# Gated delta rule on Trainium2: the old sample states of two head pairs meet their keys and queries in one visit to the tensor engine

## The chip, the cores and the metric

The kernel runs on one core of one Trainium2 chip. The metric is device time in microseconds (us) of one execution; the time before is the median of three runs, 2125.45 us (2124.71 to 2126.7). A profiled execution, from which every duration below is taken, is a run of its own.

## The reference, cut to what matters

One inference step of a one-layer hybrid decoder: 256 prompt tokens of one sequence, and 8 sample sequences of 8 tokens each. Both go through one large input projection (2048 to more than 23,000 columns), then through a gated delta rule (16 key heads, 32 value heads, state 128 x 128 for each value head) and, beside it, a sparse attention; the two are merged, projected and added to the input. The change lies in the delta rule, in the part for the sample sequences. Each of the 8 sequences brings a state S for each of 32 value heads (`state_gdn`, 8 x 32 x 128 x 128 numbers), and per chunk of tokens

```python
u = u_c - einsum('bhck,bhkv->bhcv', w_c, s)          # old state times (weighted) keys
o = einsum('bhck,bhkv->bhcv', qd_c, s) + einsum('bhij,bhjv->bhiv', qk_c, u)   # old state times queries
s = s * gt_c[..., None, None] + einsum('bhck,bhcv->bhkv', kt_c, u)
```

The products of the old state `s` with keys and with queries are what the change moves.

## The kernel before, in words

**The stream.** Nearly all the work is the multiplication of the weights of the big projections with the 320 tokens. A unit is half of the contraction (1024 of 2048) for 128 output columns. Its weights are loaded into `raw`, split by ScalarE into a rounded high part `whi` and by VectorE into the rest `wlo` (`split_ahead`, two units ahead), and multiplied by TensorE in `stream`: 16 products with `whi` (with the high and low part of the tokens in turn), then 8 with `wlo`, each 128 x 128 weights against 320 tokens. The stream's sums lie in two banks of PSUM called `pm`.

**The side work.** All else is written as Python generators. `stream` calls `side_round` twice per unit: after 12 of its 24 products, and at its end. A round steps through the list of generators once, in the order in which they were spawned; each step issues some instructions and yields. The program is thus one fixed order of instructions for each engine, settled when it is built. What decides whether a generator is stepped is a planner's clock: `Clock.cost` gives each instruction a duration, and each engine has a time.

```python
for side in list(self.sides):
    if self.pe_ns - start > limit:
        break
    if side[1] <= clock.t["tensor"]:
        self.step(side)
```

A generator that yields nothing is stepped again when the planner's tensor clock has passed the end of what it issued last, one that yields a time when that is passed. A round ends when its steps have put more than 1800 ns of products on TensorE (`pe_ns`: in `mm`, the columns of the right side divided by 2.4, times 4 for F32). A generator that takes a bank for side work (`ps`, six of them, one of which is lent to the convolution throughout this stage) goes through `need`, which also waits until a bank is idle by the planner's clock. Where a unit needs a buffer that a generator still holds, `force` runs rounds without the stream, and in these rounds banks aren't waited for.

**The recurrent stage.** The heads go by in 8 groups. A group has two head pairs; a head pair `h` is one key head with the value heads 2h and 2h+1. For each group the stream computes keys, queries, gates and values; `kq_gen` and `inverse` build the triangular inverses `XT` of the group (GpSimd works on the inverse while the stream has gone on to the next group). Then, for each head pair, four generators are in the list in this order: `v_gen` (values turned to token-major `vt`), `prompt_chain` (five steps on 256 prompt tokens), `sample_chain` and `norm_gen` (the norm over both chains' outputs `ot`, then the output gate). `G` is what the group's generators share, `K` that of a head pair. `G["T"]` appears when the group's inverse is there, and until then all chains wait.

**`sample_chain` before** (line 2144), once `G["T"]` and `vt` are there: it waits for the state tile `S` (8 sequences x 2 value heads, one DMA per value head; two such tiles in all), `vt` and `XT`; takes a bank and a tile `wt`; step 1 issues eight products, for the sequence pairs j = 0 to 3 and the parity pp of the sequence, of `R` (128 x 32: keys and queries of one sequence, the places of the other parity zero) with the state (128 x 256, both value heads). They fill partitions 32j to 32j+31 of the bank, columns 0 to 255. Two VectorE operations then form `xr` in place (`vt[:, 2]`) out of the bank, the decay `neG` and the values. Step 2 multiplies `xr` by the inverse, into the sample's part of `ot` and into `wt`. Step 3 needs four banks: products of keys with `wt`, and 16 VectorE operations that renew the state. Step 4 stores the state and gives back the tiles; when both chains of a pair have ended, `vt` is free for `v_gen` of the next group.

Below, P0 and S0 are the prompt and sample chain of a group's first head pair, P1 and S1 those of the second, and a figure behind the dot is the step: S1.3 is the state's renewal for the second pair.

In the profile each operation has the line of the common wrapper (L64), so tiles tell groups apart: `ps<-S,R` are the products that the change moves, `ps<-vt,XT` those with the inverse, `ps<-w,kq` the prompt chain's third step, `ps<-w,ktok 32*128` the renewal's products, `S<-S,gtr,ps` the renewal on VectorE. An F32 product stands as two records.

Of the kernel before, what the change touches and what calls it, by code (L numbers as in the profile page):

```python
# [12 lines left out]
OP = mybir.AluOpType  # L13
# [192 lines left out]
class Kernel:  # L206
# [1937 lines left out]
    def sample_chain(self, h, G):  # L2144
        nc, i, o = self.nc, self.i, self.o
        e, hv, K = h % 2, 2 * h, self.K[h]
        R = K["R"]
        yield from self.need(self.S)
        S = self.S.get()
        yield self.idle(S)  # L2150
        for v in range(2):
            nc.sync.dma_start(S[:, :, v, :], i["state_gdn"][0, :, hv + v].rearrange("b k v -> k b v"))
        while "T" not in G or "vt" not in K:
            yield
        vt, kt, XT = K["vt"], K["ktok"], G["XT"]
        s, stl = self.scal(G, e)
        yield self.ready(S, vt, XT)
        yield from self.need(self.ps_side)
        yield from self.need(self.w)
        xr, wt = vt[:, 2], self.w.get()  # L2160
        p = self.psum()
        for pp in range(2):
            for j in range(4):
                self.mm(p[32 * j:32 * j + 32, 0:256], R[:, 1 + pp, 32 * j:32 * j + 32], S[:, 2 * j + pp],
                        start=(pp == 0), stop=(pp == 1), skip=True)
        self.R.put(R)
        for v in range(2):
            self.stt(xr[:, v, :], p[:, 128 * v:128 * v + 128], self.neG[:, 2, hv + v:hv + v + 1], vt[:, 2, v, :],
                     OP.mult, OP.add)
        self.ps_side.put(p)  # L2170
        yield
        yield from self.need(self.ps_side)
        if "ot" not in K:
            yield from self.need(self.ot)
            K["ot"] = self.ot.get()
        ot = K["ot"]
        p = self.psum()
        for v in range(2):
            self.mm(p[:, 128 * v:128 * v + 128], XT[:, 8 + 2 * e + v, :], xr[:, v, :])
        self.act(ot[:, 2], p[:, 0:256].rearrange("p (v d) -> p v d", v=2))  # L2180
        for v in range(2):
            self.ts(wt[:, v, :], p[:, 128 * v:128 * v + 128], stl(v, 2), None, OP.mult)
        self.ps_side.put(p)
        self.drop_T(G)
        yield
        yield from self.need(self.ps_side, 4)
        ps = [self.psum() for _ in range(4)]
        for pp in range(2):
            for j in range(4):
                self.mm(ps[j][:, 256 * pp:256 * pp + 256], kt[32 * j:32 * j + 32, 2 + pp, :], wt[32 * j:32 * j + 32])  # L2190
        for j in range(4):
            for pp in range(2):
                for v in range(2):
                    bb = 2 * j + pp
                    self.stt(S[:, bb, v, :], S[:, bb, v, :], self.gtr[:, bb, hv + v:hv + v + 1],
                             ps[j][:, 256 * pp + 128 * v:256 * pp + 128 * v + 128], OP.mult, OP.add)
            self.ps_side.put(ps[j])
        yield
        for v in range(2):
            nc.sync.dma_start(o[10][0, :, hv + v].rearrange("b k v -> k b v"), S[:, :, v, :])  # L2200
        self.S.put(S)
        self.w.put(wt)
        self.drop_vt(K)
        K["S"] = True
# [296 lines left out]
```

## Time and profile before

| | before |
|---|---|
| median of 3 runs | 2125.45 us (2124.71 to 2126.7) |
| the profiled execution's own time | 2124.4 us |
| its span (first to last instruction) | 2122.7 us, mean granted TensorE clock 0.997 |
| VectorE, ScalarE, GpSimd busy | 67%, 47%, 22% of the span |
| recurrent chains, first to last state product | 878.3 to 1621.8 us |

The span is 1.7 us less than that execution's own time. In a row of the chip's profile "busy" is the time in which an engine has an instruction under way, "idle before" the idle time of the engine just ahead of the instructions of that row, with what ended it. Records of TensorE overlap, since products are pipelined; how fast they follow each other is read from their starts in the timeline.

### The profile page before, as it was taken

What the parts mean: (1) busy time and instruction counts of PE and PEld (TensorE: products, weight loads), DVE (VectorE), ACT (ScalarE), POOL (GpSimd) and SP (SyncE); (2) the same over time, 40 slices, a digit from 0 to 9 for tenths busy, and PEclk for the clock granted to TensorE, in tenths of its full rate; (3) what the DMA queues carried; (4) which work ended last, traced back from release to release, by engine and by line L of the source; (5) the groups of instructions that cost most, each with busy time, mean ns of one, the idle gap of its engine ahead of it and who ended that gap; (6) DMA issues with size and microseconds to landing.
All of it is one profiled execution on the core that took longest, in us unless ns stands there. A gap on an engine that the chain in (4) does not pass through costs nothing.

```text
span 2122.7 us, 44819 instructions
## 1 busy us (share of the span) xinstructions
PE 2093.0 (99%) x17513; PEld 2013.7 (95%) x17513; DVE 1421.5 (67%) x2900; ACT 987.5 (47%) x2253; POOL 464.3 (22%) x653
## 2 busy tenths in 40 slices
PE   7999999999999999999999999999999999999997
PEld 7999999999999999899999999999999999999997
DVE  4776655889855577777878787878666545455443
ACT  3225465333343455474747464646445534333343
POOL 2001000000001108361818181818080000000000
PEclk9999999999999999999999999999999999999998
DMA  9996663996688677686878686868687867555562
GB/s 347 333 335 179 190 177 99 289 282 183 164 240 249 197 191 202 160 235 182 226 181 228 176 232 172 232 171 228 170 246 215 246 203 210 172 152 152 161 182 81
DMA packets 713987, 438.96 MB, mean 207 GB/s; under 512 B 73936, under 2 KB 697136, under 8 KB 711472
## 3 DMA queue, kind: packets, MB, share of 16 engines
q1 hardware_dynamic: 709696, 413.45, 69.0%
q0 software_dynamic: 3616, 21.02, 2.9%
q8 instruction: 137, 2.24, 0.5%
q10 hardware_dynamic: 464, 1.65, 0.2%
q14 instruction: 74, 0.61, 0.1%
HBM read 386.81 MB, written 48.94 MB: 205 GB/s over the span
## 4 chain that ended last, share of the span: by engine, by line
PE 73%; issue 22%; DVE 2%; DMA 1%; ACT 1%; SPq 1%; DVEq 0%; POOL 0%; POOLq 0%; ACTq 0%
PE pm L64 57%; PE ps L64 16%; DMA raw<-in_w_in_dram 1%; SPq L64 1%; DVE S L64 1%; DMA rawx<-in_w_ada_dram 1%; DVE wlo L64 1%; ACT ot L64 0%; ACT whi L64 0%; DVE sga L64 0%; DVE y1l L64 0%; DVEq L2497 0%; DVE w L64 0%; DVE awl L64 0%; ACT ps L64 0%
## 5 line engine op out<-in xcount | busy, mean ns | idle before, releaser
L64 PE MATMUL pm<-xh,whi 128*128 128x320 f32 (+1 forms) x3108 | 943.5, 318 | 2.3 <-DVE qiS L64 1.3
L64 PE MATMUL pm<-xl,whi 128*128 128x320 f32 (+1 forms) x3108 | 910.4, 307 | 0.1
L64 DVE TENSOR_TENSOR wlo<-raw,whi 128x1024 fp32r<-128x1024 f32 x466 | 579.1, 1252 | 274.5 <-ACT whi L64 261.9
L64 PEld LDWEIGHTS pm<-xh,whi 128*128 128x128 f32 x3108 | 584.5, 188 | 29.8 <-issue 22.4
L64 PEld LDWEIGHTS pm<-xl,whi 128*128 128x128 f32 x3108 | 585.1, 188 | 1.3 <-DVE xl L64 0.3
L64 ACT ACTIVATE whi<-raw 128x1024 fp32r<-128x1024 f32 x466 | 489.4, 1058 | 170.6 <-PE pm L64 105.1
L64 PE MATMUL pm<-xh,wlo 128*128 128x320 f32 (+1 forms) x3108 | 521.2, 307 | 0.5 <-DVE wlo L64 0.5
L64 PEld LDWEIGHTS pm<-xh,wlo 128*128 128x128 f32 x3108 | 469.4, 188 | 1.0 <-DVE wlo L64 1.0
L64 POOL TENSOR_TENSOR X<-X,tmpx 48x31 f32<-48x31 f32 (+15 forms) x248 | 175.3, 707 | 19.4
L64 POOL TENSOR_TENSOR tmpx<-blk,X 48x31 f32<-48x31 f32 (+15 forms) x248 | 161.0, 649 | 52.3 <-DMA blk<-d_b 34.1
L64 DVE SCALAR_TENSOR_TENSOR ps<-xp,cs,ps 128x344 f32<-128x344 f32 x192 | 111.5, 581 | 6.8
L64 POOL TENSOR_TENSOR sc<-sc,mh 128x6 f32<-128x6 f32 (+1 forms) x24 | 44.4, 1848 | 276.8 <-DVE sc L64 193.7
L64 PE MATMUL pm<-y1h,whi 128*128 128x320 f32 x336 | 99.5, 309 | 1.4 <-ACT whi L64 0.9
L64 POOL TENSOR_TENSOR rfin<-rfin,mh 128x3 f32<-128x3 f32 x1 | 0.8, 849 | 455.1 <-DVE rfin L64 455.1
L64 PE MATMUL pm<-y1l,whi 128*128 128x320 f32 x336 | 99.2, 307 | 0.0
L64 DVE SCALAR_TENSOR_TENSOR S<-S,gtr,ps 128x128 f32<-128x128 f32 x256 | 67.4, 341 | 0.1
L64 PEld LDWEIGHTS pm<-y1h,whi 128*128 128x128 f32 x336 | 63.0, 187 | 1.9 <-ACT whi L64 1.9
L64 PE MATMUL ps<-xh,whi 128*128 128x320 f32 (+1 forms) x220 | 64.7, 309 | 0.0
L64 ACT ACTIVATE xp<-pm 128x256 f32<-128x256 f32 (+1 forms) x128 | 32.1, 304 | 70.1 <-PE pm L64 69.9
L64 ACT ACTIVATE ot<-ot,sc 128x128 f32<-128x128 f32 x96 | 29.9, 390 | 73.5 <-DVE sc L64 73.5
L64 PE MATMUL ps<-xl,whi 128*128 128x320 f32 (+1 forms) x220 | 63.7, 304 | 0.0
L64 PEld LDWEIGHTS pm<-y1l,whi 128*128 128x128 f32 x336 | 63.0, 187 | 0.0
(405 smaller groups left out, 2791.2 us busy)
## 6 DMA issues: line engine op xcount, KB each, us to landing
raw<-in_w_in_dram SPq DMA_DIRECT2D x328, 512.0 KB
raw<-in_w_pa_dram SPq DMA_DIRECT2D x64, 512.0 KB
rawx<-in_w_ada_dram SPq DMA_DIRECT2D x18, 1024.0 KB
a<-in_w_ada_dram SPq DMA_DIRECT2D x16, 1024.0 KB
S<-in_state_gdn_dram SPq DMA_DIRECT2D x32, 512.0 KB
out_dram<-S SPq DMA_DIRECT2D x32, 512.0 KB
raw<-in_w_pb_dram SPq DMA_DIRECT2D x32, 512.0 KB
raw<-in_w_out_dram SPq DMA_DIRECT2D x32, 512.0 KB
```

The source lines that it names most:

```text
L64: made = fn(*args, **kw)
```

## The change

Both sample chains of a group enter themselves in a list, `G["SR"]`. The first then waits for a flag, `G["xr"]`. The second waits for both state tiles and a bank, issues the eight products of the first pair into columns 0 to 255 of the bank and those of the second into columns 256 to 511, then the four VectorE operations that form both `xr`, and sets the flag. After it each chain yields until its `xr` is ready (one yield more than before), and only then takes `wt` and goes on to step 2. The number of products, of VectorE operations and of DMAs is what it was; a bank is taken once per group for them and no longer twice.

```diff
-        yield self.ready(S, vt, XT)
-        yield from self.need(self.ps_side)
+        xr = vt[:, 2]
+        G.setdefault("SR", []).append((hv, R, S, vt))
+        if len(G["SR"]) == 2:
+            yield self.ready(vt, XT, *(x[2] for x in G["SR"]))
+            yield from self.need(self.ps_side)
+            p = self.psum()
+            for c, (_, r, sv, _) in zip((0, 256), G["SR"]):
+                for pp in range(2):
+                    for j in range(4):
+                        self.mm(p[32 * j:32 * j + 32, c:c + 256], r[:, 1 + pp, 32 * j:32 * j + 32], sv[:, 2 * j + pp],
+                                start=(pp == 0), stop=(pp == 1), skip=True)
+                self.R.put(r)
+            for c, (h0, _, _, vv) in zip((0, 256), G["SR"]):
+                for v in range(2):
+                    self.stt(vv[:, 2, v, :], p[:, c + 128 * v:c + 128 * v + 128], self.neG[:, 2, h0 + v:h0 + v + 1],
+                             vv[:, 2, v, :], OP.mult, OP.add)
+            self.ps_side.put(p)
+            G["xr"] = True
+            yield
+        while "xr" not in G:
+            yield
+        yield self.ready(xr)
         yield from self.need(self.w)
-        xr, wt = vt[:, 2], self.w.get()
-        p = self.psum()
-        for pp in range(2):
-            for j in range(4):
-                self.mm(p[32 * j:32 * j + 32, 0:256], R[:, 1 + pp, 32 * j:32 * j + 32], S[:, 2 * j + pp],
-                        start=(pp == 0), stop=(pp == 1), skip=True)
-        self.R.put(R)
-        for v in range(2):
-            self.stt(xr[:, v, :], p[:, 128 * v:128 * v + 128], self.neG[:, 2, hv + v:hv + v + 1], vt[:, 2, v, :],
-                     OP.mult, OP.add)
-        self.ps_side.put(p)
-        yield
+        wt = self.w.get()
         yield from self.need(self.ps_side)
```

## The prediction

> **What bounds the kernel now.** I read the page first: busy shares, then the chain of work that ended last.
>
> ```profile
> span 2122.7 us, 44819 instructions
> PE 2093.0 (99%) x17513; PEld 2013.7 (95%) x17513; DVE 1421.5 (67%) x2900; ACT 987.5 (47%) x2253; POOL 464.3 (22%) x653
> PE 73%; issue 22%; DVE 2%; DMA 1%; ACT 1%; SPq 1%; DVEq 0%; POOL 0%; POOLq 0%; ACTq 0%
> ```
>
> TensorE is the bound: 99% busy, and other engines hold 2% of the chain or less each ("issue" is TensorE taking up its next instruction). A change is worth what it takes off TensorE's queue, plus the moments in which TensorE waits. Next, the table by stretches: the first 30 us of the chains of the second and of the last group.
>
> ```profile
> core 0: us, PE busy (x) PEld busy (x) DVE busy (x) ACT busy (x) POOL busy (x), PEclk, DMA share, GB/s
> 977.00:1007.00 30.00, 30.00 (x240) 26.98 (x239) 25.58 (x75) 14.46 (x44) 5.41 (x14) 1.00 0.64 171
> 1615.00:1645.00 30.00, 30.00 (x239) 27.06 (x238) 23.50 (x71) 17.08 (x43) 1.74 (x1) 1.00 0.77 235
> ```
>
> TensorE has no free moment there, and VectorE with 25.6 of 30 us is second, close enough to be watched. The third view is the groups of instructions:
>
> ```profile
> L64 PE MATMUL ps<-S,R 128*32 128x256 f32 x256 | 17.1, 385 | 0.0
> ```
>
> 256 records are 128 products, 16 visits of eight. 17.1 us is all that they are busy, so even their removal would be 0.8% of the run; they are only regrouped. "Busy" doesn't show what a visit costs, though: for that I take TensorE's timeline, the first group's two visits.
>
> ```profile
> 877.78 0.60 PE L64 MATMUL ps<-vt,XT 128*128 128x128 f32 x4
> 878.32 1.07 PE L64 MATMUL ps<-S,R 128*32 128x256 f32 x16
> 879.32 0.42 PE L64 MATMUL pm<-xh,whi 128*128 128x320 f32 x1
> 879.57 0.31 PE L64 MATMUL pm<-xl,whi 128*128 128x320 f32 x1
> ...
> 881.04 0.31 PE L64 MATMUL pm<-xl,whi 128*128 128x320 f32 x1
> 881.18 0.59 PE L64 MATMUL ps<-w,ktok 128*128 128x256 f32 x2
> 881.61 0.61 PE L64 MATMUL ps<-vt,PT 128*128 128x128 f32 x4
> 882.06 1.06 PE L64 MATMUL ps<-vt,XT 128*128 128x128 f32 x8
> 883.04 1.07 PE L64 MATMUL ps<-S,R 128*32 128x256 f32 x16
> 884.04 0.41 PE L64 MATMUL pm<-xh,whi 128*128 128x320 f32 x1
> 884.30 0.31 PE L64 MATMUL pm<-xl,whi 128*128 128x320 f32 x1
> ```
>
> Prices from starts: the stream makes ten products from 879.57 to 881.04, 0.147 us each. Two records of 256 columns take 881.18 to 881.61, 0.216 each; four of 128 columns 881.61 to 882.06, 0.11 each.
>
> **What a visit of the state products costs.** From the first `vt,XT` (877.78) to the second product of the resumed stream (879.57) are 1.79 us. Four records of 128 columns (0.44) and one of the stream (0.147) leave 1.20 for the state products. In the second visit: 884.30 less 882.06 is 2.24, less eight records (0.88), less 0.147, leaves 1.21. What should they take? Their products use 32 columns of the array, so four run side by side, and narrow windows of the timeline show that they start in fours:
>
> ```profile
> 878.32 0.42 PE L64 MATMUL ps<-S,R 128*32 128x256 f32 x4
> 878.56 0.61 PE L64 MATMUL ps<-S,R 128*32 128x256 f32 x8
> 878.77 0.61 PE L64 MATMUL ps<-S,R 128*32 128x256 f32 x8
> ```
>
> The fours start at 878.32, 878.56 and 878.77, some 0.22 apart, the pace of one 256-column record, and that with other weights each time. Four fours at 0.216 are 0.86. So 0.34 us of each visit is a surcharge for going into the 32-column form and out of it: a late start (878.32, where the fourth `vt,XT` record would end at 878.22), a late return, and 0.25 instead of 0.147 to the stream's second product. Is it paid by any interruption of the stream? No:
>
> ```profile
> 895.04 0.31 PE L64 MATMUL pm<-xl,whi 128*128 128x320 f32 x1
> 895.18 1.02 PE L64 MATMUL ps<-w,kq 128*128 128x256 f32 x4
> 895.86 0.50 PE L64 MATMUL pm<-xh,whi 128*128 128x320 f32 x1
> 896.19 0.30 PE L64 MATMUL pm<-xl,whi 128*128 128x320 f32 x1
> ```
>
> From 895.18 to 896.19 are 1.01; less 0.147 that is 0.86, four records at 0.216 and nothing over. Full-width side work interrupts the stream for free; the narrow form is what costs.
>
> **The change part by part.** *Merged visit.* All 16 products now follow each other: eight fours at 0.216 (1.73) and one surcharge (0.34), 2.07 in place of 2.41. Saved: 0.34 a group, 2.7 us over 8 groups. Bounds: nothing, if going from the first pair's half to the second's costs a surcharge too; 2.5 if the fours' own pace of 0.22 is taken. I take 2.7, since fours already follow each other at that pace from one sequence to the next.
>
> [...]
>
> *When it is issued.* In the first round (877.78) the old order was P0.1, S0.1, and then the round's 1800 ns were used up (eight products count 3413), so P1.1 and S1.1 came a round later (882.06, 883.04). Now S0 issues nothing, so P1.1 (427) follows P0.1 (427), and S1 issues the merged visit, all in the first round. Its conditions hold there: inverse and values are the same for both pairs, and the states were loaded long before. The first pair's VectorE operations wait for the whole visit, 0.86 later; nothing of that pair is due before the next round anyway.
>
> *What follows.* The added yield puts S0.2 one round later, into the third with P0.3 and P1.3. Then: fourth round P0.4, S0.3; fifth P0.5, P1.4, S1.2; sixth P1.5 and, if four banks are free, S1.3. Before, it took nine rounds. Fewer rounds save nothing by themselves (above), but the chains end some 5 to 8 us sooner: a round is 12 products (1.76) and the side work. VectorE's and ScalarE's operations are as many as before, the DMAs too; SyncE's state loads and stores only move with the chains. The later `wt` and the two `R` tiles given back together hold nobody up.
>
> *The stall in the first group.* Here something late today may come early enough:
>
> ```profile
> 898.77 1.15 PE L64 MATMUL ps<-w,ktok 32*128 32x256 f32 x16
> 901.11 0.44 PE L64 MATMUL ps<-ident,vf 128*128 128x128 f32 x2 [0.53 <-DVE S L64]
> 902.14 0.66 PE L64 MATMUL ps<-ident,vf 128*128 128x128 f32 x4 [0.60 <-DVE S L64]
> ```
>
> The stream needs a value buffer, `force` runs the side work alone, S1.3 goes out (898.77), and `v_gen` of the next group waits twice for VectorE to empty S1.3's banks: 1.13 us. `v_gen` needed `vt` of the first pair, free only after P0.5 in this same round. With P0.5 two rounds sooner nothing need be forced. I take the 1.13; bounds are 0 and the same again, if the early order only moves the forced rounds elsewhere.
>
> *The sum.* 2.7 and 1.1 are 3.8 us off the profiled execution's own 2124.4: 2120.6. The median of the runs shown is 1.05 above that execution, so in the median's terms 2125.45 - 3.8 = 2121.6, or 0.18% less. A measurement of this kernel tells about 0.2% (4.25 us) from no change.
>
> **Rivals.** *More stalls go (faster by over 0.2%).* Two later waits of TensorE have ScalarE late with `whi`, behind a norm's operations:
>
> ```profile
> 1550.57 0.41 PE L64 MATMUL pm<-xh,whi 128*128 128x320 f32 x1 [0.30 <-ACT whi L64]
> 1654.33 0.41 PE L64 MATMUL pm<-y1h,whi 128*128 128x320 f32 x1 [0.87 <-ACT whi L64]
> ```
>
> Norms follow chains, so chains that end sooner may take both away: 3.8 + 1.2 = 5.0, 2120.4. For it: both rows name a `whi` that stands behind a norm on ScalarE, and the norm would go earlier. Against: an order that is new everywhere may put its own waits there.
>
> *VectorE is overrun (slower).* Before, the renewals S0.3 and S1.3 were 14.5 us apart, now about 7:
>
> ```profile
> 986.87 1.15 PE L64 MATMUL ps<-w,ktok 32*128 32x256 f32 x16
> 1001.33 1.15 PE L64 MATMUL ps<-w,ktok 32*128 32x256 f32 x16
> 983.24 1.20 DVE L64 TENSOR_SCALAR w<-ps,sc 128x128 f32<-128x128 f32 x4 [2.58 <-ACT ot L64]
> 988.16 4.21 DVE L64 SCALAR_TENSOR_TENSOR S<-S,gtr,ps 128x128 f32<-128x128 f32 x16
> 1004.42 4.22 DVE L64 SCALAR_TENSOR_TENSOR S<-S,gtr,ps 128x128 f32<-128x128 f32 x16
> 1010.37 1.87 ACT L64 ACTIVATE ot<-ot,sc 128x128 f32<-128x128 f32 x6 [5.36 <-DVE sc L64]
> 1013.21 1.05 ACT L64 ACTIVATE whi<-raw 128x1024 fp32r<-128x1024 f32 x1
> 1014.60 0.31 PE L64 MATMUL pm<-xh,whi 128*128 128x320 f32 x1
> ```
>
> The place is the norm after S1.3: ScalarE waits 5.36 us for VectorE's small operation, which stands behind the renewal, and `whi` behind that ends (1014.26) only 0.34 before TensorE needs it (1014.60). VectorE, busy 25.6 of 30, has some 1.0 us free in 7; 4.2 of renewal is then 3.2 us late. If half of that reaches `whi`, 1.6 less 0.34 is 1.3 us of stall in each of 8 groups: 10 - 2.7, 2132.8. It begins to cost from 0.34 us of delay on, and shows as slower from (4.25 + 2.7) / 8 = 0.87 of stall a group. Against it: the work moves forward, into VectorE's idle time (2.58 at 983.24), and at that time ScalarE waits for VectorE, so an earlier renewal also lets the norm go earlier. [...] In the visit itself the rows speak against it: four operations after 2.07 us of products, at the renewal's pace (4.21 for 16) 1.1 us.
>
> *Only the surcharge goes:* 2.7, 2122.75. *It doesn't do what it says:* the halves pay a surcharge each, or S1 isn't ready in the first round and nothing else shifts: 2125.45 at worst.
>
> **How the numbers follow.** Forecast case 0.40; only the surcharge 0.16; more stalls gone 0.30; nothing saved 0.06; VectorE overrun 0.08. The forecast lies 0.45 us short of the bound, and the runs shown spread over 2 us, so I count 0.06 of its 0.40 as faster by over 0.2%: faster 0.36, same 0.56, slower 0.08. The range reaches on the one side to the case of more stalls, with the second bound of the forced rounds (2120.4 - 1.1, so 2119.3), on the other to nothing saved and one us of spread, 2126.5.
>
> **What would show it right or wrong.** In the profile after, `ps<-S,R` must stand in the timeline as x32, eight times, with 2.07 us between the end of full-width work and the resumed pace; 2.4 would show a surcharge between the halves. Ahead of it should stand eight `vt,XT` records, of P0.1 and P1.1. `ident,vf` should have no idle time before it. VectorE overrun would show as idle time of `pm<-xh,whi` or `pm<-xh,wlo` after `whi` or `wlo`, group after group some 35 us after the visit. I am wrong in the step of the rounds if chains end no sooner, and in the main term if the span changes by less than 2 us with every wait as it was.

## The result, and the profile after

| | before | after |
|---|---|---|
| median | 2126.15 us (2124.71 to 2127.02, 6 runs) | 2140.11 us (2139.16 to 2140.67, 6 runs) |
| span of the profiled execution | 2122.7 us | 2137.5 us |
| granted clock, mean | 0.997 | 0.995 |

The change makes the kernel slower by 14.0 us: ratio 1.0066, 95% interval 1.0057 to 1.0076. The forecast was 2121.6 us, the range 2119.3 to 2126.5; the result lies outside it, on the other side.

The page of the kernel after, its head and the shares of the chain of work that ended last:

```profile
span 2137.5 us, 44793 instructions
PE 2099.1 (98%) x17513; PEld 2021.3 (95%) x17513; DVE 1421.6 (67%) x2900; ACT 987.5 (46%) x2253; POOL 463.6 (22%) x653
PE 66%; issue 22%; DVE 6%; DMA 3%; ACT 2%; SPq 1%; DVEq 0%; POOL 0%; POOLq 0%; ACTq 0%
```

The counts of TensorE's, VectorE's, ScalarE's and GpSimd's instructions are those of before to the last one, and VectorE is busy as long. No work was added. What changed is the chain: VectorE holds 6% of it in place of 2%, DMA 3% in place of 1%. TensorE now waits for others.

**The merged visit** is there, eight times. The first group's, in TensorE's timeline of the kernel after (start, duration, engine, line, operation, records):

```profile
878.15 1.05 PE L64 MATMUL ps<-vt,XT 128*128 128x128 f32 x8
879.13 1.93 PE L64 MATMUL ps<-S,R 128*32 128x256 f32 x32
880.99 0.41 PE L64 MATMUL pm<-xh,whi 128*128 128x320 f32 x1
881.24 0.31 PE L64 MATMUL pm<-xl,whi 128*128 128x320 f32 x1
```

From 878.15 to 881.24 are 3.09 us; eight records at 0.11 and one of the stream (0.147) taken off leave 2.06. The price was 2.07, and the other seven visits come to the same.

**The waits of TensorE** in the stage (from 740 us to its end), of the kernel after: who waits, for whom, us in all, how often, the longest.

```profile
PE pm L64 <- ACT whi L64: 7.6, 6, 2.6
PE ps L64 <- DMA cst<-in_conv_w_dram: 2.5, 2, 2.3
PE ps L64 <- DVE S L64: 1.1, 3, 0.6
PE pm L64 <- DVE wlo L64: 0.7, 2, 0.4
PE ps L64 <- DVE w L64: 0.4, 2, 0.2
```

The same view of the kernel before:

```profile
PE pm L64 <- ACT whi L64: 1.2, 2, 0.9
PE ps L64 <- DVE S L64: 1.1, 2, 0.6
PE pm L64 <- DVE M L64: 0.5, 1, 0.5
```

12.3 us in place of 2.8, so 9.5 more. The stream stands still for its weights `whi` six times, and once for 2.3 us for a small table `cst` of the convolution. The place of the longest wait, in the second group, by the timelines of four engines of the kernel after:

```profile
1013.23 4.21 DVE L64 SCALAR_TENSOR_TENSOR S<-S,gtr,ps 128x128 f32<-128x128 f32 x16
1017.36 0.17 DVE L64 COPY ct<-xp 128x27 f32<-128x27 f32 x1
1017.46 0.56 DVE L64 TENSOR_SCALAR ps<-xp,cs 128x344 f32<-128x344 f32 x1
1018.05 1.81 DVE L64 SCALAR_TENSOR_TENSOR ps<-xp,cs,ps 128x344 f32<-128x344 f32 x3
1019.78 0.65 DVE L64 TENSOR_TENSOR sc<-sc,sc 128x6 f32<-128x6 f32 x1
1011.78 1.32 POOL L64 TENSOR_TENSOR sc<-sc,mh 128x6 f32<-128x6 f32 x1 [3.43 <-DVE sc L64]
1020.46 1.86 ACT L64 ACTIVATE ot<-ot,sc 128x128 f32<-128x128 f32 x6 [6.11 <-DVE sc L64]
1022.23 1.99 ACT L64 ACTIVATE whi<-raw 128x1024 fp32r<-128x1024 f32 x2
1023.32 0.42 PE L64 MATMUL pm<-xh,whi 128*128 128x320 f32 x1 [2.58 <-ACT whi L64]
```

Read it from the bottom up. TensorE waits 2.58 us for `whi`. `whi` stands on ScalarE behind the norm's six operations on `ot`, and these waited 6.11 us for VectorE's small operation on `sc` (128 x 6 numbers). What that needs, GpSimd's power, has been there since 1013.10; but on VectorE it stands behind the 16 renewals of S1.3 and a convolution. Work of 0.65 us, late by 6.7, holds up two engines.

### The profile page after: what moved, and what is told of

Same layout as the page of the kernel before. It is cut to its first block, busy times and chain, and to the rows that moved or that the text cites. A ratio compares the mean times of both kernels' runs of the same rounds, so it can differ in the third digit from the quotient of the medians.

```text
span 2137.5 us, 44793 instructions
## 1 busy us (share of the span) xinstructions
PE 2099.1 (98%) x17513; PEld 2021.3 (95%) x17513; DVE 1421.6 (67%) x2900; ACT 987.5 (46%) x2253; POOL 463.6 (22%) x653
## 4 chain that ended last, share of the span: by engine, by line
PE 66%; issue 22%; DVE 6%; DMA 3%; ACT 2%; SPq 1%; DVEq 0%; POOL 0%; POOLq 0%; ACTq 0%
PE pm L64 51%; PE ps L64 16%; DVE S L64 2%; DVE wlo L64 1%; DVE ps L64 1%; DMA raw<-in_w_in_dram 1%; DMA rawx<-in_w_ada_dram 1%; ACT whi L64 1%; SPq L64 1%; DMA raw<-in_w_ada_dram 0%; ACT ot L64 0%; DVE w L64 0%; DMA cst<-in_conv_w_dram 0%; DMA c<-in_c_sample_dram 0%; DVE sc L64 0%
## 5 line engine op out<-in xcount | busy, mean ns | idle before, releaser
L64 POOL TENSOR_TENSOR X<-X,tmpx 48x31 f32<-48x31 f32 (+15 forms) x248 | 184.4, 744 | 19.4
L64 POOL TENSOR_TENSOR tmpx<-blk,X 48x31 f32<-48x31 f32 (+15 forms) x248 | 156.3, 630 | 91.3 <-DMA blk<-d_b 73.3
L64 ACT ACTIVATE ot<-ot,sc 128x128 f32<-128x128 f32 x96 | 29.9, 390 | 79.8 <-DVE sc L64 79.8
```

Source lines behind the costliest of these rows:

```text
L64: made = fn(*args, **kw)
```

## The experiments

Each time is a median beside runs of the kernel before on the same chip (2125.7 to 2126.12 us), with the ratio to it and its interval. The letters in the recorded expectations are those of the theories as they stood then; ahead of each run its theory is given by what it says.

**The norm's small operation, in both kernels.** The theory: ScalarE's wait for that one VectorE operation is what stops the stream. The edit puts it on GpSimd right behind the power; the planner is shown the old operation at the old place, so that nothing else changes its order.

```diff
         self.tt(m[:, 12:18], m[:, 6:12], self.mh.to_broadcast([128, 6]), OP.pow, eng=nc.gpsimd)
+        nc.gpsimd.engine.tensor_tensor(mv(12), mv(12), qf, OP.mult)
         yield
-        self.tt(mv(12), mv(12), qf, OP.mult)
+        self.emitted += 1
+        self.clock.enter("vector", "tensor_tensor", (mv(12), mv(12), qf, OP.mult), {})
```

> The changed kernel; in norm_gen the one small multiplication of the norm's factors (128 x 6) is made by GpSimd, right behind its power, instead of by VectorE behind whatever stands there; the order of every other instruction is that of the changed kernel. Theory A (the changed order puts the second pair's renewal of 16 VectorE operations ahead of that multiplication, ScalarE waits for it with the next weights' high part queued behind, and TensorE runs dry): the idle time of TensorE ahead of pm<-xh,whi after ACT whi falls from 7.6 us to below 1.5 us, and the time from 2140.1 to 2127 to 2130. Theory B (the merged visit itself, or its place in the round, costs the time): no change, 2139 to 2141.

> The kernel before with the same multiplication moved to GpSimd; the control of the run e1. Theory A: before, TensorE waited only 1.2 us for whi in the recurrent stage, so it gains 0.5 to 2 us: 2124 to 2125.7. Theory B: no change, 2125.5 to 2126.7. If both e1 and e2 lose some 14 us the run e1 says nothing.

In the kernel after: 2129.82 us, ratio 1.0017 (1.0008 to 1.0027), 10.3 us back. In the kernel before: 2122.65, ratio 0.9984 (0.9974 to 0.9993), 3.5 less, more than expected; 1.2 of it stands in the trace as waits of TensorE that are gone (1.6 us in place of 2.8), and where the rest comes from is open. The waits of TensorE in the edited kernel after, the three largest, and the place from above on ScalarE:

```profile
PE ps L64 <- DMA cst<-in_conv_w_dram: 3.5, 2, 2.7
PE ps L64 <- DMA X<-d_x: 2.3, 4, 1.0
PE ps L64 <- DVE S L64: 1.1, 3, 0.6
```

```profile
1013.28 1.86 ACT L64 ACTIVATE ot<-ot,sc 128x128 f32<-128x128 f32 x6
1015.04 2.00 ACT L64 ACTIVATE whi<-raw 128x1024 fp32r<-128x1024 f32 x2
```

The norm starts without a wait, `whi` is made some 6 us earlier (7.2 by the rows, but this run is 0.95 ahead at the operations before the norm already), and no wait for `whi` is left in the whole stage. So the mechanism is shown. Its size: 3.5 of the 10.3 are to be had without the change as well, so the new order's own loss at this place is 6.8 us. With the edit in both kernels, after still stands 7.2 us above before.

**Less renewal ahead of it.** The same theory from the other end: leave the small operation where it is and shorten what stands ahead. The renewal for the second pair works on 8 of 128 columns; the rest of that state isn't renewed.

```diff
+                    full = (S[:, bb, v, :], S[:, bb, v, :], self.gtr[:, bb, hv + v:hv + v + 1],
+                            ps[j][:, 256 * pp + 128 * v:256 * pp + 128 * v + 128])
+                    if e == 0:
+                        self.stt(*full, OP.mult, OP.add)
+                        continue
+                    nc.vector.engine.scalar_tensor_tensor(
+                        S[:, bb, v, 0:8], S[:, bb, v, 0:8], full[2],
+                        ps[j][:, 256 * pp + 128 * v:256 * pp + 128 * v + 8], op0=OP.mult, op1=OP.add)
+                    self.emitted += 1
+                    self.clock.enter("vector", "scalar_tensor_tensor", full, dict(op0=OP.mult, op1=OP.add))
```

> The changed kernel; the 16 VectorE operations that renew the second pair's state work on 8 of 128 columns (the rest of that state isn't renewed: part of the computation is left out); the order of all instructions is that of the changed kernel, and the products are unchanged. Theory A: the renewal shortens from 4.2 us to about 2 us, ScalarE's wait for the norm's factors shortens by 2 us a group, and TensorE's idle time after ACT whi falls from 7.6 to 1 to 3 us: 2129 to 2133. Theory B: 2139 to 2141.

2130.82 us, ratio 1.0023 (1.0013 to 1.0033): 9.3 us back, and the waits for `whi` fall from 7.6 to 1.9 us, ScalarE's for the small operation from 79.8 to 68.2 (in a profiled execution of 2134.97 us, some 4 above the median). S1.3's renewal is what the small operation stands behind.

**The added yield.** The theory (C): one yield more per chain makes the order worse; the merge as such doesn't. Taken out of after:

```diff
         while "xr" not in G:
             yield
-        yield self.ready(xr)
```

and put alone into before, where nothing is merged:

```diff
         self.ps_side.put(p)
         yield
+        yield self.ready(xr)
```

> The changed kernel without the added yield until xr is ready: both sample chains go on to the product with the inverse as soon as the planner steps them again. The order of everything behind it changes. Theory C (the added yield puts the first pair's renewal a round or more later, and with it the second pair's and the norm): the second renewal comes within 24 us of the merged visit, as it came within 24 us of the first visit before, and the time is 2121 to 2126. Theory A says only that the time goes with TensorE's waits for whi: 2123.4 plus those waits beyond the 1.2 us of before. Theory B: 2139 to 2141.

> The kernel before, products in two visits as they were, with the added yield alone (each sample chain waits until its xr is ready before it goes on). Theory F (any shift of the order upsets what is next to the narrow margin of whi, merged visit or not): 2130 or more. Theory C in its weaker form (the yield costs a round in the chain): 2127 to 2130. Theory G (the loss needs the merged visit, which brings both pairs to the same point at once): 2125 to 2127.

After without it: 2139.01 us, ratio 1.0057 (1.0041 to 1.0074), so the yield isn't the cause; the waits are of another make-up (`whi` 5.4, `cst` 3.1, and 2.5 for VectorE's `M`). S0.3 now comes 9.6 us behind the group's first `vt,XT`, near the 9.1 of before, but in the second group S1.3 still comes 28.4 us behind it, where the theory had it within 24. Before with it: 2143.58, ratio 1.0085 (1.0068 to 1.0102). This kernel merges nothing and adds no instruction to any engine's work, and yet it loses 17.7 us, more than the change: 7.0 of `whi`, 4.7 of `cst`. A theory in which one part of the change is to blame falls with that; left is that the order itself is (F).

**Both, the yield out and the small operation on GpSimd:**

> The kernel of e4 (the changed kernel without the added yield) with the small multiplication on GpSimd. Theory A: TensorE's waits for whi, 5.4 us in e4, go, and the time falls from 2139.0 to 2128 to 2132; it beats e2 (2122.65) only if the waits for cst (3.1 us in e4) go as well.

2128.45 us, ratio 1.0011 (1.0001 to 1.002). The waits for `whi` are gone here too; the largest that is left is one of 5.0 us for `cst`.

**The wait for `cst`.** The theory (D): on SyncE's one queue the state loads, now issued just ahead of the small loads, delay them. SyncE's timeline, after and before, at the small loads for which TensorE waits 2.3 us in after:

```profile
1253.81 4.81 SPq L64 DMA_DIRECT2D S<-in_state_gdn_dram  x2
1258.67 1.75 SPq L64 DMA_DIRECT2D cst<-in_state_conv_dram  x1
```

```profile
1235.84 1.02 SPq L64 DMA_DIRECT2D S<-in_state_gdn_dram  x2
1240.66 2.63 SPq L64 DMA_DIRECT2D cst<-in_state_conv_dram  x1
```

In both kernels, counted from the first of each, the same two state loads stand ahead of the same `cst`. After, they take 4.81 us to issue, `cst` follows at once, and TensorE is ready for it 4.1 us after its issue began (1258.67 to 1262.75). Before, they took 1.02, and TensorE came to `cst` 7.3 us after its issue began (at 1247.95), without a wait. The experiment stands on the kernel after with the GpSimd edit, and from the third head pair on loads one sequence of eight:

```diff
-            nc.sync.dma_start(S[:, :, v, :], i["state_gdn"][0, :, hv + v]...)
+            n = 8 if h < 2 else 1
+            nc.sync.engine.dma_start(S[:, 0:n, v, :], i["state_gdn"][0, 0:n, hv + v]...)
+            self.clock.enter("sync", "dma_start", ...)
```

> The kernel of e1 (the changed kernel with the norm's small multiplication on GpSimd); from the third head pair on, the loads of the sample states bring one sequence of eight (part of the computation is left out); the order of all instructions is that of e1. Theory D (what e1 still loses beside e2 is mostly SyncE's one queue: the state loads, now issued just ahead of the next group's convolution inputs, delay those, and TensorE waits for them at the transposes of cst and at the inverse): TensorE's waits for DMA cst and DMA X, 6.3 us together in e1, fall below 2 us, and the time goes from 2129.8 to 2122 to 2126. Rival (the wait is SyncE's own, for the earlier part of its queue, and not for the loads' bytes): 2129 to 2130.5.

2127.66 us, ratio 1.0004 (0.9994 to 1.0014): each beside its own runs of before, 1.9 less than with the full loads, short of what was expected, and the two intervals overlap. The waits for `cst` are gone, but 3.4 us of waits for `X`, another small load, remain. So the theory holds for `cst`, and not for all of the DMA waits. The time that the two state loads take to issue can hardly be what delayed `cst`, and their size doesn't set it: with an eighth of the bytes they still take 4.13 us at this place (4.55 with all of them, in the kernel after with the GpSimd edit), while the first issue of `cst` falls from 1.75 to 0.39. What makes these issues long here stays open.

**A product of full width between the two halves,** in after, to test the price of the narrow form:

```diff
             for c, (_, r, sv, _) in zip((0, 256), G["SR"]):
+                if c:
+                    nc.tensor.engine.matmul(p[:, 256:384], XT[:, 0, :], vt[:, 0, 0, :], start=True, stop=True, ...)
```

> The changed kernel; between the first pair's eight state products and the second pair's stands one product of full width (128 x 128 weights, 128 columns), whose result is overwritten. The price of the narrow form is tested: by it (0.34 us for going in and out of the 32-column form) the visit, 2.07 us from the end of the full-width work to the resumed pace, grows by 0.34 and by the added product's own 0.22, to 2.63 us; if going in and out is free or is paid once per visit whatever stands in it, it grows by 0.22 to 2.29. The time: 2140 to 2144.6, as far as TensorE's later waits don't take it up.

2145.79 us, ratio 1.0094 (1.0077 to 1.0111). TensorE's timeline:

```profile
878.12 1.05 PE L64 MATMUL ps<-vt,XT 128*128 128x128 f32 x8
879.10 1.07 PE L64 MATMUL ps<-S,R 128*32 128x256 f32 x16
880.10 0.49 PE L2165 MATMUL ps<-vt,XT 128*128 128x128 f32 x2
880.52 1.07 PE L64 MATMUL ps<-S,R 128*32 128x256 f32 x16
881.52 0.41 PE L64 MATMUL pm<-xh,whi 128*128 128x320 f32 x1
881.77 0.31 PE L64 MATMUL pm<-xl,whi 128*128 128x320 f32 x1
```

From 878.12 to 881.77 are 3.65 us, 0.56 more than after's 3.09. The added product's two records are 0.22 of that; 0.34 is what going out of the narrow form and into it again costs, the surcharge of the prediction; all eight visits show the same. The time is 1.2 us above the range that was expected.

**The merge alone, in before's order.** If the order is to blame, the same merged visit without a new order must bring the 2.7 us. Before, with S0.1's step issuing both pairs' products and the four VectorE operations, while the planner is shown the two visits at their old places:

```diff
+        G.setdefault("SR", []).append((hv, R, S, vt))
...
+        for c, (_, r, sv, _) in zip((0, 256), G["SR"] if both and first else []):
+            for pp in range(2):
+                for j in range(4):
+                    nc.tensor.engine.matmul(p[32 * j:32 * j + 32, c:c + 256], r[:, 1 + pp, 32 * j:32 * j + 32], sv[:, 2 * j + pp], ...)
...
-                self.mm(*a, start=(pp == 0), stop=(pp == 1), skip=True)
+                self.pe_ns += 256 / 2.4 * 4
+                self.emitted += 1
+                self.clock.enter("tensor", "matmul", a, dict(start=(pp == 0), stop=(pp == 1), skip_group_check=True))
```

> The kernel before with the merged visit alone: the second pair's eight state products follow the first pair's in the same visit and bank, its two VectorE operations follow the first pair's; the planner is shown the two visits of before, so the order of everything else is that of before, instruction for instruction. The price theory (0.34 us saved a group by one way in and out of the narrow form instead of two): 2.7 us less, 2122.7 to 2123.9, and the second visit is gone from the timeline. Rival (the merged visit costs something of its own, in VectorE's wait for the whole bank or in the burst of 2.07 us): 2126 or more.

2123.04 us, ratio 0.9987 (0.9978 to 0.9996): 2.7 us less than before (2125.70). Its visit in TensorE's timeline:

```profile
878.08 0.60 PE L64 MATMUL ps<-vt,XT 128*128 128x128 f32 x4
878.62 1.93 PE L2171 MATMUL ps<-S,R 128*32 128x256 f32 x32
880.48 0.42 PE L64 MATMUL pm<-xh,whi 128*128 128x320 f32 x1
880.73 0.31 PE L64 MATMUL pm<-xl,whi 128*128 128x320 f32 x1
```

2.65 us less four records (0.44) and 0.147 are 2.06 again. The interval leaves 0.9 to 4.7 us for the gain; that it is 2.7 rests on the visits in the timeline as well. Here TensorE's waits are those of before, to 0.4 us in all. And with the small operation on GpSimd as well:

> The kernel of e9 with the norm's small multiplication on GpSimd, as in e2. If the two gains are apart from each other: 2122.65 of e2 less 2.7, that is 2119.5 to 2120.5. If ScalarE's and VectorE's waits were hidden under what the merged visit saves: 2121.5 to 2123.

2119.89 us, ratio 0.9974 (0.9964 to 0.9984): the two gains (2.7 and 3.5) add up to 5.8 of 6.2. This version is faster than both kernels.

**Another order, and nothing else.** The last test of F: before, with the planner's fixed cost of a VectorE operation changed by 3% from the start of this stage on. `self.nudge` is 0.165 in the one kernel and 0.155 in the other; no instruction is added, removed or altered.

```diff
-                return 0.16 + n * (0.0006 if fast and sb else 0.00106)
+                return self.nudge + n * (0.0006 if fast and sb else 0.00106)
```

> The kernel before with no change in its work: from the recurrent stage on, the planner's fixed part of a VectorE operation is 0.165 in place of 0.16 us, so that the order from there on is another. Theory F (the order of before is a favourable one with margins of tenths of a us, and nearly any other order costs 5 us or more): 2131 or more. Rival (a nudge of no meaning costs nothing much, and what e7 and the changed kernel lose belongs to the sample chains' own order): 2124 to 2129.

> As e11 with 0.155 us. Theory F: 2131 or more. Rival: 2124 to 2129.

0.165: 2135.28 us, ratio 1.0047 (1.0031 to 1.0062). 0.155: 2138.96, ratio 1.0065 (1.005 to 1.0081). Their waits of TensorE, the first row of each:

```profile
PE pm L64 <- ACT whi L64: 9.8, 8, 1.6
```

```profile
PE pm L64 <- ACT whi L64: 5.9, 5, 4.3
```

9.6 and 13.3 us are lost, with `whi` ahead again. In the first kernel the chain from above is there with nothing merged: ScalarE's operations on `ot` wait 4.83 us for VectorE's small operation (until 1128.19), which stands behind a renewal (1121.37), and TensorE then waits 1.31 for `whi`. In the second, 4.3 of the 5.9 us are one wait of another make-up: ScalarE stood idle for 9.1 us ahead of an operation on `zf` (962.14), and its row doesn't say what ended that. Five other orders of this work (these two, the added yield in before, the change with it and without) all cost between 9.6 and 17.7 us, the 2.7 saved counted in. Among the six it is before's order that stands out.

## Why the prediction was wrong, step by step

**The bound** was read rightly: TensorE's queue sets the time (busy 99% of the span before, 98% after), and most of the loss that could be placed is TensorE waiting (9.5 us).

**The price of the merged visit** was right in all its terms: 2.06 for 2.07 us, the surcharge 0.34 (full width between the halves), 2.7 us over eight groups (merge alone). The halves share one surcharge, so the bound "nothing" and the rival in which it doesn't do what it says are out.

**The first round** went as worked out: eight `vt,XT` records, then the visit.

**"The chains end some 5 to 8 us sooner" is the step that failed,** and with it the sum, which gave the new order no price: by the runs it costs 16.7 us. The renewals in TensorE's timeline of the kernel after, with the visit's first row:

```profile
982.35 1.05 PE L64 MATMUL ps<-vt,XT 128*128 128x128 f32 x8
1000.31 1.15 PE L64 MATMUL ps<-w,ktok 32*128 32x256 f32 x16
1010.61 1.15 PE L64 MATMUL ps<-w,ktok 32*128 32x256 f32 x16
```

and the start of the second group before:

```profile
977.80 0.60 PE L64 MATMUL ps<-vt,XT 128*128 128x128 f32 x4
```

S1.3 comes 28.3 us behind the first `vt,XT` (982.35 to 1010.61); before it was 23.5 (977.80 to 1001.33). Over the eight groups S1.3 comes 0.9 to 5.4 us later than before, in none sooner. S0.3, which before came 9.1 us behind the first `vt,XT` in seven groups, now comes 12.7 to 18.0 us behind it. In the third group the round count holds for S0.3 (1080 to 1093), and S1.3 follows 15.6 us behind it. The prediction gave the condition itself, "if four banks are free", and then counted as if they were. Without the added yield S0.3 is back at 9.6 us and S1.3 still late, so the yield holds S0.3 back and not S1.3. By the code, S1.3 has to find four idle banks at once, and other generators take them one by one; that this is what kept it back is argued, no run tested it alone.

**"The stall in the first group" was not gone.** The forced waits in after, at the same operation:

```profile
903.49 0.44 PE L64 MATMUL ps<-ident,vf 128*128 128x128 f32 x2 [0.16 <-DVE S L64]
904.52 0.96 PE L64 MATMUL ps<-ident,vf 128*128 128x128 f32 x4 [0.60 <-DVE S L64]
```

With 0.34 at the renewal's own products it is 1.10 in place of 1.13: the bound 0, nothing gained. By the code it hung on the failed step: in this group S0.3 comes 18.0 us behind the first `vt,XT` (878.15 to 896.11), twice the 9.1 of before, and `vt` comes free only when this chain too has ended.

**"SyncE's state loads and stores only move with the chains"** failed as well: `cst` came late in after, and `X` too in the kernel after with the GpSimd edit, though at the place of the longest such wait the queue's order of state loads and `cst` is that of before.

**The rivals.** The two late waits for `whi` whose end the rival with more gain foresaw are gone: counted in the stream's order, the same two products start at 1563.52 and 1670.37 without one. But one unit later than the first and two units ahead of the second stand new waits, 1.4 us (until 1568.56) and 2.4 (until 1662.98) in place of 0.30 and 0.87; that a new order may put its own waits there was the rival's own objection. "VectorE is overrun" had the right place and the right chain: renewal, the norm's small operation, ScalarE's `ot`, `whi`. Its trigger was wrong (renewals 7 us apart; they are 10.3 and 15.6 apart in the second and third group), and so was its chance, 0.08. Its price of 10 us in all was nearer: 7.6 us of waits for `whi`, to which came 2.5 for `cst` and a granted clock of 0.50 in three stretches of 3.41 us that nobody had foreseen (below). The row with the 0.34 us of margin stood in the prediction. It was read as one place at which one thing might go wrong. With the runs of other orders it reads as a sign that this order lives on margins of tenths, and that a new order draws them anew.

**The sum in the trace.** 9.5 us more of waits and an estimated 4.6 of slower products (below), less the 2.7 saved, are 11.4 of the 14.8 us between the two spans; 3.4 us could not be put down to places. By the runs instead: the visit saves 2.7, so the order costs 16.7, 6.8 of it through the norm's small operation. 9.9 are left with the GpSimd edit in both kernels; the trace of after with that edit shows 6.3 us of waits for `cst` and `X` and a mean granted clock of 0.996, beside the 0.997 of before with it. What makes before's order so good, and how the losses of the other orders divide, stays open.

## What to carry to other kernels

Where the order of instructions is fixed when the program is built, an edit of one part is two edits, the work and the order: price them apart, by issuing the new work in the old order, and by a change of the planner that alters no work, which shows how much an order alone is worth. In the profile of before, look for small operations on which an engine waits with something needed soon queued behind it (here 5.36 us of waiting and 0.34 of margin), and move them to an engine that is free: that gained 3.5 us here before the change was made. Counting rounds didn't give the time of a step that needs several buffers at once: here it came later in all eight groups, where the count had it sooner.

## What the runs showed of the hardware

In the kernel after, TensorE was granted half its clock for a while behind two of its three waits of 2.3 us and more in the stage. The table by stretches, around the wait for `cst` that ends at 1265.06:

```profile
core 0: us, PE busy (x) PEld busy (x) DVE busy (x) ACT busy (x) POOL busy (x), PEclk, DMA share, GB/s
1260.00:1265.00 5.00, 2.75 (x20) 2.48 (x18) 2.48 (x8) 5.00 (x16) 4.29 (x10) 1.00 1.14 289
1265.06:1266.54 1.48, 1.48 (x11) 1.48 (x12) 1.44 (x3) 1.48 (x7) 1.32 (x3) 1.00 1.19 291
1266.55:1269.96 3.41, 3.41 (x15) 3.41 (x14) 3.40 (x12) 2.82 (x6) 3.03 (x6) 0.50 1.04 317
1269.97:1275.00 5.03, 5.03 (x38) 5.03 (x37) 4.68 (x8) 0.29 (x2) 2.12 (x4) 1.00 0.70 165
```

For 1.5 us TensorE goes on at full pace; then the granted clock is 0.50 for 3.41 us, in which the stream's products follow each other at 0.266 us, not 0.147. After has three such stretches in the stage, 10.2 us in all; before has none. By an estimate from the two paces each loses 3.41 x (1 - 0.147 / 0.266), or 1.5 us, the three together 4.6. So behind the wait of 2.31 us some 1.5 us more were lost, which no view of waits shows.

The slow stretches begin at 904.73, 1024.20 and 1266.55 us. The second starts 0.9 us behind the wait of 2.58 us for `whi` that ends at 1023.32. The first stands behind waits of 1.10 us in all, those of the first group; before has 1.13 us of them (0.53 and 0.60) in its first group and no slow stretch behind them. From 1269.97 to the end of the stage the granted clock of after is 1.00, behind the waits of 1.36 us (until 1568.56) and 2.38 us (until 1662.98) too. The length of a wait alone thus doesn't tell what it costs here. From each start to the next are 35 and 71 times 3.413 us; whether the cost of a wait depends on where it falls against this beat, no run tested.
